# A two-layer trunk with stick-breaking attention: pairs of heads summed at once, gated outputs' low halves on GpSimd, side products dealt by VectorE's work, 72 z products one chunk later

## The chip, the cores and the metric

The kernel runs on one core of one Trainium2 chip. The metric is the time of one execution on the device, in microseconds. An execution has TensorE (PE, with its weight loads PEld), VectorE (DVE), ScalarE (ACT), GpSimd (POOL) and the DMA queue of SyncE (SP). Each engine takes its instructions in order and waits by semaphore.

## What is computed

Two layers on a sequence of 2048 tokens, 1024 channels, all in float32. Layer A is a pooling mixer with a SiLU gate, then an output projection, a residual and a gated embedding add. Layer B is attention with 16 heads of 64 channels. Keys and values come from a projection of the stream after layer A. For layer B, cut to what matters here:

```python
h = rms_norm(x, b_norm[j])
q, z = jnp.split(h @ b_w_in[j], 2, axis=-1)
q = rms_norm(split_heads(q), b_q_norm[j])
# A[t,s] = beta[t,s] * prod_{s<j<t} (1 - beta[t,j]), beta = sigmoid(q.k / sqrt(d)), s < t
o = stick_breaking_attention(q, k_sh, v_sh)
x = x + (o * jax.nn.silu(z)) @ b_w_out[j]
x = x + (p[i] @ ple_w[i]) * jax.nn.sigmoid(x @ ple_gate_w[i])
```

## The kernel before

**Products in two halves.** Every operand of a product with a weight is kept as a pair: a rounded high half and a low half, the rest that the rounding left. A product is three matmuls for each 128 channels of depth: high by high, low by high, high by low (`piecewise`, L990). So each such operand costs a copy on ScalarE (the high half) and a subtraction on VectorE or GpSimd (the low half).

**First part, up to about 1333 us.** Layer A and the projections to q, k and v run for the four chunks of 512 tokens one after the other. Their results go to memory. The change leaves this part as it is: the instructions of every engine keep their order there.

**Second part, the attention.** The four chunks of queries are taken from the last to the first (chunk 3 to chunk 0). In a chunk the heads 0 to 15 follow each other, and for a head the key chunks from its own down to 0. One (query chunk, head, key chunk) is a slot; each slot has four steps, one for each 128 queries. There are 640 steps, numbered n through the loop at L1133: chunk 3 has steps 0 to 255, chunk 2 the steps 256 to 447, chunk 1 the steps 448 to 575, chunk 0 the rest. A head has 16, 12, 8 or 4 steps.

A step does this, in three places of the program:

- `front` (L917): two matmuls give 128x512 logits (L924, L925), ScalarE takes the sigmoid (L928), and VectorE makes the running product along the keys with a scan (L936; for the head's own key chunk L933, where only the keys up to the queries' tile count, so that its four steps are 128, 256, 384 and 512 wide). The scan's two inputs both lie in SBUF.
- six steps later, `turn` (L943): four transposes on TensorE (L949) into one of two PSUM buffers `psa`, a rounded copy by ScalarE (L952) and the low half by VectorE (L953), which reads the PSUM buffer and frees it.
- two steps after that, `gather` (L956): two matmuls (L961, L962) add to the head's output in PSUM (`pso`).

**The end of a head.** A PSUM output holds two 64-row halves that have to be added. One step after the head's last gather, ScalarE copies one half to its place in `os` (L976), and a step later VectorE adds the other half from PSUM (L977). After the odd head of a pair, `gated` adds a vector to the pair with four ScalarE instructions (L972) and GpSimd multiplies by silu(z) (L974). Later `pair_up` (L1000) makes the pair's high half on ScalarE (L1005) and its low half on VectorE (L1006).

**Side products.** Between the steps the loop takes matmuls from a second stream, `filler`, at a fixed number a step (L1152 to L1155). In chunk 3 these are the z products of all four chunks (`gate_z`, L1009: 192 matmuls for a query chunk, 8 groups of 24, and for each group one VectorE multiplication at L1026 and one GpSimd multiplication at L1031). In chunk 2 it is `post(3)` (L1041): chunk 3's output projection (192 matmuls), then its gate and embedding (8 groups of 31). In chunk 1 it is `post(2)`, in chunk 0 `post(1)`, and after the last step `post(0)` runs alone, as the tail. When a chunk's eighth pair is done, 14 steps after its last, what is left of the stream is flushed and the next stream begins (L1166 to L1173). `soon(k, ...)` puts a piece of work k steps later; `stay` holds an instruction at its place in the written order.

Of the kernel before, what the change touches and what calls it, by code (L numbers as in the profile page):

```python
# [15 lines left out]
P = 128  # L16
# [6 lines left out]
W5 = 512  # L23
# [12 lines left out]
def trunk_kernel(ctx, tc, x, xt, pt0, wut, cols, heads, zin, grp, aout, agate, aple,  # L36
# [819 lines left out]
    with ExitStack() as st:  # L856
# [99 lines left out]
        def gather(st, kt):  # L956
# [6 lines left out]
            if st["last"] and kt == 3:  # L963
                half, os, c, h2 = st["h"] % 2, st["os"], st["c"], st["h"] // 2
                mine, other = slice(half * HD, (half + 1) * HD), slice((1 - half) * HD, (2 - half) * HD)

                def gated():
                    zt = t2.tile([P, W5], F32, tag="zt", name="zt", bufs=1)
                    nc.sync.dma_start(out=zt, in_=zd[c][h2])
                    for j in range(4):  # L970
                        js = slice(j * P, (j + 1) * P)
                        stay(A.activation(out=os[:, js], in_=os[:, js], func=AF.Identity,  # L972
                                          bias=ends[c][:, h2, j : j + 1]))
                    G.tensor_tensor(out=os, in0=os, in1=zt, op=ALU.mult)  # L974

                soon(1, lambda: stay(A.copy(out=os[mine], in_=po[other])))  # L976
                soon(2, lambda: V.tensor_tensor(out=os[mine], in0=po[mine], in1=os[mine], op=ALU.add))  # L977
# [22 lines left out]
        def pair_up(c):  # L1000

            if len(ogs[c]) < len(outs[c]):
# [3 lines left out]
                soon(1, lambda: V.tensor_tensor(out=pr[:, 1], in0=os, in1=f(pr[:, 0]), op=ALU.subtract))  # L1006
# [31 lines left out]
        POSTZ = 8 * 24  # L1038
        POST = 8 * 24 + 8 * 31 + 2
# [59 lines left out]

        def beside(c):  # L1100

            if c < NSUB - 1:
                yield from post(c + 1)
                return
            for cz in range(c, -1, -1):
                yield from gate_z(cz)
# [11 lines left out]
        rate = POSTZ / 64.0 - AHEAD * LAG_T / 256.0  # L1118
# [3 lines left out]
        def begin(i):  # L1122
            c, h, kc = slots[i]
            if kc == c:
                if h == 1:
                    early["ends"] = load_ends(c)
                os = head["os"] if h % 2 else t2.tile([P, W5], F32, tag="os", name="os", bufs=9)
                head.clear()
                head.update(q=early.pop("q", None) or load_q(c, h), carry=[None] * 4, o=[], os=os)
# [3 lines left out]
        for n in range(4 * len(slots) + LAG_G):  # L1133
# [18 lines left out]
            owed += rate + (AHEAD if n < LAG_T else 0)  # L1152
# [13 lines left out]
            for c in range(NSUB - 1, 0, -1):  # L1166
                if len(outs[c]) == 8 and c not in done:
# [4 lines left out]
                    rate = POST / (64.0 * c - (LAG_G + 2 if c == 1 else 1))  # L1172
# [57 lines left out]
```

## Time and profile before

| | |
|---|---|
| median of 3 runs | 2716.79 us (2716.16 to 2717.45) |
| the profiled execution, its own time | 2715.51 us |
| its span, first to last instruction | 2713.6 us |
| granted TensorE clock, mean | 0.999 |
| busy over the span | PE 2681.3 us (99%), PEld 2224.8 (82%), DVE 1967.6 (73%), ACT 1365.9 (50%), POOL 874.5 (32%) |
| DMA | 581.55 MB, 214 GB/s |

The profile counts from the span's start. Its stages: the first part 0 to 1333 us, chunk 3 to 1835, chunk 2 to 2183, chunk 1 to 2432, chunk 0 to about 2600, the tail to the end. A row of the windows view gives the busy time of each engine in a stretch. PE's busy time is a union of matmuls whose ends are modelled and which lie over the next one's start, so that a short stop of TensorE does not show in it in full; PEld, the weight loads, is the second witness. A row of a group view ends with the idle time that the engine had just before such instructions, and with what ended it.

### The profile page before, as it was taken

Reading aid. Unit: us, or ns where it says so; the run is one execution under the profiler, and the core shown is the slowest. Engines: PE = TensorE matmul, PEld = TensorE weight load, DVE = VectorE, ACT = ScalarE, POOL = GpSimd, SP = SyncE. Lnnn points to the kernel's source line nnn. Section 1 sums busy time; section 2 is a strip of 40 time slices with the busy share of each in tenths; the row PEclk is TensorE's granted clock in tenths of the full one; section 3 lists DMA queues with packets and bytes.
Section 4 is the critical chain, followed back from the end, with each engine's and each line's share of the span. In section 5 each row is a group of like instructions: output and inputs, shape, how many; then the busy total and the mean of one; then the engine's idle time right before and its main releaser. Section 6 shows DMA issues by size and latency. Waiting matters only on the chain.

```text
span 2713.6 us, 38599 instructions
## 1 busy us (share of the span) xinstructions
PE 2681.3 (99%) x13352; PEld 2224.8 (82%) x13352; DVE 1967.6 (73%) x2565; ACT 1365.9 (50%) x2671; POOL 874.5 (32%) x695
## 2 busy tenths in 40 slices
PE   9999999999999999999999999999999999999999
PEld 8888888888888888888888888887887778888877
DVE  6776626665367643765499999999999998997632
ACT  5445513455135642445365666666666665655430
POOL 3675238642485325753211111110110111112220
PEclk9999999999999999999999999999999999999999
DMA  8657785567846677445679665555555566668865
GB/s 326 225 179 274 249 297 188 208 232 261 295 169 239 222 259 274 136 157 188 201 246 289 187 221 166 169 171 164 178 158 160 164 198 203 197 197 261 268 226 171
DMA packets 276543, 581.55 MB, mean 214 GB/s; under 512 B 33110, under 2 KB 66902, under 8 KB 276348
## 3 DMA queue, kind: packets, MB, share of 16 engines
q1 hardware_dynamic: 270610, 571.41, 63.9%
q10 hardware_dynamic: 5738, 7.68, 1.0%
q8 instruction: 106, 1.74, 0.3%
q14 instruction: 89, 0.73, 0.1%
HBM read 438.40 MB, written 132.19 MB: 210 GB/s over the span
## 4 chain that ended last, share of the span: by engine, by line
PE 85%; DVE 10%; issue 2%; DMA 2%; ACT 1%; POOL 0%; SPq 0%; ACTq 0%; DVEq 0%; POOLq 0%
PE psd L614 19%; PE psd L166 9%; PE psd L167 9%; PE psd L168 9%; PE psa L949 7%; PE psd L993 5%; PE psd L995 5%; PE psd L997 5%; DVE pp L936 5%; PE pso L962 3%; PE psl L925 3%; PE pso L961 3%; PE psl L924 3%; DVE at L953 3%; PE pst L719 1%
## 5 line engine op out<-in xcount | busy, mean ns | idle before, releaser
L952 ACT CAST at<-psa 128x512 fp32r<-128x512 f32 (+3 forms) x640 | 334.8, 523 | 480.4 <-PE psa L949 463.8
L614 PE MATMUL psd<-wpair,x 128*128 128x512 f32 x2304 | 536.8, 391 | 0.0
L936 DVE TENSOR_TENSOR_SCAN pp<-kap,pp,zeros 128x512 f32<-128x512 f32 x384 | 514.2, 1339 | 3.1 <-ACT kap L928 2.4
L614 PEld LDWEIGHTS psd<-wpair,x 128*128 128x128 f32 x2304 | 429.8, 188 | 87.1
L953 DVE TENSOR_TENSOR at<-psa,at 128x512 fp32r<-128x512 f32 (+3 forms) x640 | 380.9, 595 | 83.2 <-ACT at L952 80.3
L949 PE MATMUL psa<-ident,pp 128*128 128x128 f32 x2176 | 346.9, 275 | 21.4 <-DVE at L953 20.2
L928 ACT ACTIVATE kap<-psl 128x512 f32<-128x512 f32 (+3 forms) x640 | 345.2, 539 | 14.2 <-PE psl L925 11.2
L949 PEld LDWEIGHTS psa<-ident,pp 128*128 128x128 f32 x2176 | 262.8, 140 | 98.1 <-DVE at L953 45.8
L924 PE MATMUL psl<-kk,qa 128*128 128x512 f32 (+3 forms) x640 | 281.9, 441 | 0.0
L962 PE MATMUL pso<-at,vv 128*128 128x512 f32 (+3 forms) x640 | 234.7, 367 | 0.8 <-DVE at L953 0.8
L925 PE MATMUL psl<-kk,qb 128*128 128x512 f32 (+3 forms) x640 | 232.7, 364 | 0.0
L961 PE MATMUL pso<-at,vv 128*128 128x512 f32 (+3 forms) x640 | 231.9, 362 | 0.0
L933 DVE TENSOR_TENSOR_SCAN pp<-kap,ahead 128x128 f32<-128x128 f32 (+3 forms) x256 | 223.0, 871 | 5.3 <-ACT kap L928 3.9
L167 PE MATMUL psd<-xp,wpair 128*128 128x512 f32 x512 | 199.4, 390 | 1.5 <-DVE xp L316 1.5
L166 PE MATMUL psd<-xp,wpair 128*128 128x512 f32 x512 | 199.9, 391 | 0.0
L168 PE MATMUL psd<-xp,wpair 128*128 128x512 f32 x512 | 199.2, 389 | 0.0
L149 DVE SCALAR_TENSOR_TENSOR wpair<-wraw,gains,wpair 128x512 fp32r<-128x512 f32 x192 | 161.4, 882 | 45.8 <-ACT wpair L148 45.1
L1031 POOL TENSOR_TENSOR zr<-zr,sgz 128x512 f32<-128x512 f32 x32 | 58.9, 1840 | 370.0 <-ACT sgz L1030 326.9
L143 POOL TENSOR_TENSOR wpair<-wraw,wpair 128x512 fp32r<-128x512 f32 x99 | 144.4, 1468 | 81.2 <-ACT wpair L141 76.6
L148 ACT ACTIVATE wpair<-wraw,gains 128x512 fp32r<-128x512 f32 x192 | 132.9, 718 | 69.3 <-DMA wraw<-in_bq_dram 29.6
L141 ACT CAST wpair<-wraw 128x512 fp32r<-128x512 f32 x148 | 89.7, 618 | 119.5 <-PE psd L168 91.4
L962 PEld LDWEIGHTS pso<-at,vv 128*128 128x128 f32 x640 | 120.2, 188 | 27.9 <-DVE at L953 1.5
(194 smaller groups left out, 5318.8 us busy)
## 6 DMA issues: line engine op xcount, KB each, us to landing
kk<-kd SPq DMA_DIRECT2D x320, 128.0 KB
vv<-vd SPq DMA_DIRECT2D x160, 256.0 KB
wraw<-in_kv_dram SPq DMA_DIRECT2D x128, 256.0 KB
wpair<-wzd SPq DMA_DIRECT2D x64, 512.0 KB
wpair<-wod SPq DMA_DIRECT2D x64, 512.0 KB
wpair<-wgd SPq DMA_DIRECT2D x64, 512.0 KB
wpair<-wu SPq DMA_DIRECT2D x48, 512.0 KB
wpair<-wi SPq DMA_DIRECT2D x36, 512.0 KB
```

What stands on the lines that cost most here:

```text
L166: T.matmul(ps, wst(units, kt, 0, c0), acts[kt][:, 0], start=(begin and kt == order[0]), stop=False)
L167: T.matmul(ps, wst(units, kt, 0, c0), acts[kt][:, 1], start=False, stop=False)
L168: T.matmul(ps, wst(units, kt, 1, c0), acts[kt][:, 0], start=False, stop=(end and kt == order[-1]))
L614: T.matmul(pss2[i], ck["x2"][kt][:, xh, tk], wst(ws, kt, wh, 0, W5), start=(kt == 0 and xh == 0 and wh == 0), stop=(kt == KT - 1 and wh == 1))
L924: T.matmul(ps[:, :w], qa[:, qs], kk[:, :w], start=True, stop=False)
L925: T.matmul(ps[:, :w], qb[:, qs], kk[:, :w], start=False, stop=True)
L928: A.activation(out=kp[:, r0:], in_=ps[:, :w], func=AF.Sigmoid, scale=-1.0)
L936: V.tensor_tensor_scan(out=pp[:, ::-1], data0=kp[:, ::-1], data1=zeros.to_broadcast([P, W5]), initial=st["carry"][j], op0=ALU.mult, op1=AL ...
L949: T.transpose(pt[:, j * P : (j + 1) * P], pp[:, r0 + kt * P : r0 + (kt + 1) * P], ident)
L952: A.copy(out=at[:, 0, cs], in_=pt[:, cs])
L953: V.tensor_tensor(out=at[:, 1, cs], in0=pt[:, cs], in1=f(at[:, 0, cs]), op=ALU.subtract)
L962: T.matmul(po[:, cs], vv[:, kt, :], at[:, 1, cs], start=False, stop=(st["last"] and kt == 3))
```

## The change

Four edits, all in the attention part.

**Heads.** At the end of a head both halves are now copied from PSUM by ScalarE: the half in the wrong rows to a second buffer `ob` (L976), the other to `os` (L977). VectorE adds only once for a pair of heads, 128x512 from SBUF and SBUF (L979), in place of two additions of 64x512 from PSUM and SBUF. `gated` comes one step later than before.

**Low halves.** `pair_up`'s subtraction is on GpSimd (L1007), but for the two that fall in the tail, which stay on VectorE.

**Side products dealt.** In chunks 3 and 2 the number of side products of a step is no longer fixed. `shares` works out from the widths of a step's scan and low half a time for VectorE, and from its matmuls one for TensorE, and gives each step as many side products as bring TensorE's time to k times VectorE's, at least 0.5; k is found so that the sum is right. The dealing goes on to 14 steps past the chunk's last (step 269, then 461). Chunks 1 and 0 keep a fixed number.

**72 products later.** The z products of chunk 0 are begun in chunk 3 as before, but 72 of their 192 matmuls (3 of 8 groups) are left over and come first in chunk 2. Chunk 3 then has 696 side products in place of 768, chunk 2 has 514 in place of 442.

```diff
             if st["last"] and kt == 3:
-                half, os, c, h2 = st["h"] % 2, st["os"], st["c"], st["h"] // 2
+                half, os, ob, c, h2 = st["h"] % 2, st["os"], st["ob"], st["c"], st["h"] // 2
...
-                soon(2, lambda: V.tensor_tensor(out=os[mine], in0=po[mine], in1=os[mine], op=ALU.add))
+                soon(1, lambda: stay(A.copy(out=ob[mine], in_=po[other])))
+                soon(2, lambda: stay(A.copy(out=os[mine], in_=po[mine])))
                 if half:
-                    soon(3, gated)
+                    soon(3, lambda: V.tensor_tensor(out=os, in0=os, in1=ob, op=ALU.add))
+                    soon(4, gated)
                     soon(6, lambda: outs[c].append(os))
...
-                soon(1, lambda: V.tensor_tensor(out=pr[:, 1], in0=os, in1=f(pr[:, 0]), op=ALU.subtract))
+                soon(1, lambda: (V if tail[0] else G).tensor_tensor(
+                    out=pr[:, 1], in0=os, in1=f(pr[:, 0]), op=ALU.subtract))
...
+        HELD = 3 * 24
...
+        last_z = gate_z(0)
...
         def beside(c):
...
+            if c == NSUB - 1:
+                for cz in range(c, 0, -1):
+                    yield from gate_z(cz)
+                for _ in range(POSTZ - HELD):
+                    next(last_z)
+                    yield
                 return
...
+            if c == NSUB - 2:
+                yield from last_z
+            yield from post(c + 1)
...
+        def widths(n, lag):
+            i, j = divmod(n - lag, 4)
+            if not 0 <= i < len(slots):
+                return 0
+            c, _, kc = slots[i]
+            return (4 if kc < c else (j + 1 if not lag else 4 - j)) * P
...
+        def shares(n0, n1, total):
+            scan, turned_, gathered = ([widths(n, lag) for n in range(n0, n1)] for lag in (0, LAG_T, LAG_G))
+            vector = [(0.15 + 0.0022 * a if a else 0.0) + (0.14 + 0.00105 * t if t else 0.0) for a, t in zip(scan, turned_)]
+            tensor = [2 * max(0.109, 0.2265 * a / W5) * (a > 0) + 0.109 * t / P + 2 * max(0.109, 0.2265 * g / W5) * (g > 0)
+                      for a, t, g in zip(scan, turned_, gathered)]
+            part = lambda k: [max(0.5, (k * v - t) / 0.2265) + (AHEAD if n0 + i < LAG_T else 0)
+                              for i, (v, t) in enumerate(zip(vector, tensor))]
...
-        rate = POSTZ / 64.0 - AHEAD * LAG_T / 256.0
+        share, even = shares(0, stops[NSUB - 1], NSUB * POSTZ - HELD), 0.0
...
-            owed += rate + (AHEAD if n < LAG_T else 0)
+            owed += even or share.get(n, 0.0)
...
-                    rate = POST / (64.0 * c - (LAG_G + 2 if c == 1 else 1))
+                    if c == NSUB - 1:
+                        share = shares(n + 1, stops[c - 1], POST + HELD)
+                    else:
+                        even = POST / (64.0 * c - (LAG_G + 2 if c == 1 else 1))
```

Two places where the order of instructions moves. The first is TensorE at the passage from chunk 3 to chunk 2. `xz` is the z products' input, so a row with `xz` is a side product; L924 with 128x128 is the first step of chunk 2. Before, TensorE has there:

```order
L993 MATMUL psd<-xz,wpair 128x512
L995 MATMUL psd<-xz,wpair 128x512
L997 MATMUL psd<-xz,wpair 128x512
L961 MATMUL pso<-at,vv 128x512
L962 MATMUL pso<-at,vv 128x512
L949 MATMUL psa<-ident,pp 128x128 x4
L924 MATMUL psl<-kk,qa 128x128
L925 MATMUL psl<-kk,qb 128x128
L961 MATMUL pso<-at,vv 128x512
L962 MATMUL pso<-at,vv 128x512
L949 MATMUL psa<-ident,pp 128x128 x4
L924 MATMUL psl<-kk,qa 128x256
```

Now it has, a little further on in the same head, from its second step:

```order
L924 MATMUL psl<-kk,qa 128x256
L925 MATMUL psl<-kk,qb 128x256
L998 MATMUL psd<-xz,wpair 128x512
L961 MATMUL pso<-at,vv 128x512
L962 MATMUL pso<-at,vv 128x512
L949 MATMUL psa<-ident,pp 128x128 x4
L924 MATMUL psl<-kk,qa 128x384
L925 MATMUL psl<-kk,qb 128x384
L994 MATMUL psd<-xz,wpair 128x512
L996 MATMUL psd<-xz,wpair 128x512
```

Before, the side products end with the last step of chunk 3, and the first ones of the next stream come 14 steps later; now nearly every step from there on has one to four.

The second place is ScalarE at the end of an odd head of chunk 2. `kap` is the sigmoid's output, L952 the rounded copy that VectorE's L953 needs. Before:

```order
L976 COPY os<-pso 64x512
L952 CAST at<-psa 128x128
L928 ACTIVATE kap_12443<-psl 128x512
L952 CAST at<-psa 128x512
L928 ACTIVATE kap_12444<-psl 128x512
L972 ACTIVATE os<-os,en 128x128 x4
```

Now, at the end of such a head:

```order
L976 COPY ob<-pso 64x512
L952 CAST at<-psa 128x128
L928 ACTIVATE kap_12443<-psl 128x512
L977 COPY os<-pso 64x512
L952 CAST at<-psa 128x512
L928 ACTIVATE kap_12444<-psl 128x512
L952 CAST at<-psa 128x512
L928 ACTIVATE kap_12445<-psl 128x512
L972 ACTIVATE os<-os,en 128x128 x4
```

One more copy stands ahead of a step's L952, and the four instructions of `gated` come one step later.

More of the change, by code (lines that the diff above doesn't have):

```diff
@@ L1117, in trunk_kernel @@
         AHEAD = 4
-        rate = POSTZ / 64.0 - AHEAD * LAG_T / 256.0
+        stops = {}
+        for n, (c, _, _) in enumerate(slots):
+            stops[c] = 4 * (n + 1) + LAG_G + 6
+        share, even = shares(0, stops[NSUB - 1], NSUB * POSTZ - HELD), 0.0
         done = set()
@@ L1127, in begin @@
                 os = head["os"] if h % 2 else t2.tile([P, W5], F32, tag="os", name="os", bufs=9)
+                ob = head["ob"] if h % 2 else t2.tile([P, W5], F32, tag="ob", name="ob", bufs=1)
                 head.clear()
[L1129 removed]
+                head.update(q=early.pop("q", None) or load_q(c, h), carry=[None] * 4, o=[], os=os, ob=ob)
             kk = early["k"].pop(0) if early["k"] else load_k(kc, h)
```

10 lines of the change are left out of this document (5 added, 5 removed).

## The prediction

> **What bounds the kernel now.** I read the page's busy times first, then the windows view, cut at the chunks of the attention, with chunk 2 (1835 to 2183) cut in three. Each of its rows gives, after a stretch's length, the busy time and count of PE, PEld, DVE, ACT and POOL.
>
> ```profile
> PE 2681.3 (99%) x13352; PEld 2224.8 (82%) x13352; DVE 1967.6 (73%) x2565; ACT 1365.9 (50%) x2671; POOL 874.5 (32%) x695
> ```
>
> ```profile
> 1333.00:1835.00 502.00, 496.77 (x2701) 412.98 (x2700) 473.36 (x565) 300.90 (x599) 76.55 (x44) 1.00 0.66 205
> 1835.00:1860.00 25.00, 21.14 (x121) 15.46 (x120) 24.91 (x32) 17.80 (x38) 2.56 (x2) 1.00 0.65 198
> 1860.00:2032.00 172.00, 171.52 (x957) 143.11 (x956) 169.96 (x213) 111.58 (x229) 24.14 (x13) 1.00 0.53 163
> 2032.00:2183.00 151.00, 142.64 (x779) 115.67 (x778) 148.58 (x185) 93.19 (x191) 11.52 (x8) 1.00 0.53 163
> 2183.00:2432.00 249.00, 245.27 (x1350) 205.02 (x1349) 230.93 (x305) 150.40 (x329) 37.17 (x24) 1.00 0.66 202
> 2432.00:2600.00 168.00, 167.68 (x892) 141.42 (x891) 118.90 (x184) 82.70 (x202) 35.41 (x24) 1.00 0.83 253
> ```
>
> TensorE is the bound nearly everywhere: it is idle for 5.2, 3.9, 0.5, 8.4, 3.7 and 0.3 us, 22.0 in all. VectorE is nearly full in chunk 2 (24.91 of 25, 148.58 of 151). Next the waits view of the attention, TensorE's two rows: what waited, for what, us, times, longest.
>
> ```profile
> PEld psa L949 <- DVE at L953: 45.8, 72, 2.6
> PE psa L949 <- DVE at L953: 20.2, 35, 2.2
> ```
>
> So one thing stops TensorE: a transpose finds no free PSUM buffer because VectorE has not yet taken the low half out of it. The matmul view understates these stops, since a row's end lies over the next start. Three stretches without a stop show it by the weight loads:
>
> ```profile
> 1500.00:1725.00 225.00, 225.00 (x1233) 188.22 (x1232) 211.91 (x254) 135.83 (x269) 32.27 (x18) 1.00 0.58 185
> 1862.00:1955.00 93.00, 92.92 (x517) 77.80 (x518) 91.69 (x116) 59.97 (x123) 12.30 (x7) 1.00 0.56 174
> 2220.00:2350.00 130.00, 130.00 (x720) 110.15 (x719) 118.90 (x155) 77.80 (x170) 21.50 (x13) 1.00 0.66 198
> ```
>
> Where TensorE never stops, PEld is busy 188.22/225 = 0.8365 of the time, 0.847 in chunk 1. A stretch's PEld over that share is its full work: 493.7 of 502, 18.5 of 25, 171.1 of 172, 138.3 of 151, 242.0 of 249. By this the idle time is 8.3, 6.5, 0.9, 12.7 and 7.0, with chunk 0's 0.3 together 35.7 us. The Trainium skill, "Perfetto Trace Analysis", section "Identifying the Most-Contended Engine", says the same of the witness: judge TensorE's headroom by weight-load time, not by matmul busy time. By that page alone PEld's 82 to 84% would promise a sixth of the span; the trace disagrees, since 0.8365 is what a stretch without any stop has.
>
> The change keeps every one of the 13352 matmuls. What it can win is therefore these 22 to 36 us, no more.
>
> **z products, 72 of them, and the dealing.** A side product's price, from a stretch of ten back to back in the tail, first and last:
>
> ```profile
> 2610.77 0.40 PE L993 MATMUL psdt<-og,wpair 128*128 128x512 f32 x1
> ...
> 2612.82 0.39 PE L993 MATMUL psdt<-og,wpair 128*128 128x512 f32 x1
> ```
>
> Nine intervals take 2.05 us, 0.228 each. So 72 x 0.228 = 16.4 us of TensorE's work leave chunk 3 and enter chunk 2: on the sum nothing, unless they land where TensorE stood idle. They do: in 1835 to 1860, 14 steps, TensorE had no side products at all, and is given some 37 (8.4 us) against 3.9 to 6.5 us idle. I count that idle as gone but for 0.5 to 1. Chunk 1's first 14 steps likewise get some 37 of chunk 2's.
>
> The rest depends on VectorE's demand beside TensorE's. These are VectorE's rows of chunk 2, by form, and the last the scan of chunk 3:
>
> ```profile
> L936 DVE TENSOR_TENSOR_SCAN pp<-kap,pp,zeros 128x512 f32<-128x512 f32 x128 | 171.9, 1343 | 0.3 <-ACT kap L928 0.2
> L977 DVE TENSOR_TENSOR os<-pso,os 64x512 f32<-64x512 f32 x16 | 10.8, 678 | 0.2
> L1006 DVE TENSOR_TENSOR og<-os,og 128x512 fp32r<-128x512 f32 x7 | 5.6, 806 | 0.0
> L1085 DVE TENSOR_TENSOR sg<-sg,x 128x512 f32<-128x512 f32 x6 | 4.0, 660 | 0.0
> L1026 DVE TENSOR_TENSOR zr<-psd,rb 128x512 f32<-128x512 f32 x1 | 0.7, 657 | 0.0
> ...
> L936 DVE TENSOR_TENSOR_SCAN pp<-kap,pp,zeros 128x512 f32<-128x512 f32 x192 | 257.8, 1343 | 2.6 <-ACT kap L928 2.3
> ```
>
> **Heads.** Sixteen additions (10.8 us) become eight. Before has no such addition; the nearest rows with two SBUF inputs and this shape are L1085 (0.660) and, stretched at times, L1006 (0.806). I take 0.70: 5.6 us, so 5.2 saved a chunk (bounds 4.4 and 5.5).
>
> **Low halves on GpSimd.** Eight a chunk leave VectorE, 8 x 0.806 = 6.4 us. They don't leave it wholly. One place, with what GpSimd does beside:
>
> ```profile
> 2157.82 1.29 POOL L1084 TENSOR_TENSOR sg<-sg,x 128x512 f32<-128x512 f32 x1 [25.22 <-DVE sg L1083]
> 2158.26 1.93 DVE L936 TENSOR_TENSOR_SCAN pp<-kap,pp,zeros 128x512 f32<-128x512 f32 x1
> 2159.06 2.19 POOL L974 TENSOR_TENSOR os<-os,zt 128x512 f32<-128x512 f32 x1
> 2160.11 1.68 DVE L1006 TENSOR_TENSOR og<-os,og 128x512 fp32r<-128x512 f32 x1
> 2162.45 0.66 PE L949 MATMUL psa<-ident,pp 128*128 128x128 f32 x4 [2.19 <-DVE at L953]
> ```
>
> And the durations of scan and low half over all steps, minimum, median and maximum in ns:
>
> ```profile
> L936 DVE TENSOR_TENSOR_SCAN pp<-kap,pp,zeros x384: 1262/1275/2330, 1341.7 to 2432.6; 128x512 f32<-128x512 f32 x192
> L953 DVE TENSOR_TENSOR at<-psa,at x640: 257/659/694, 1345.8 to 2609.3; 128x512 fp32r<-128x512 f32 x160
> ```
>
> Beside GpSimd the scan takes 1.93 in place of its median 1.275, L1006 1.68, and TensorE stops for 2.19 us. The two rows above show who is hit: the scan, both inputs in SBUF, goes up to 2.33; L953, one input in PSUM, never past 0.69. The Trainium skill, "GPSIMD Engine Reference", section "Key points", has this as a rule: GpSimd shares its SBUF interfaces with VectorE and contends with instructions of two SBUF inputs. The trace agrees by 2.33 against 0.69. It speaks against this change twice: more GpSimd work beside the scans, and L977, with a PSUM input, gives way to an addition that can be hit.
>
> The mean price: scans exceed their median by 1.343 - 1.275 = 0.068; times 128 that is 8.7 us in chunk 2, over GpSimd's 23 instructions 0.38 each; chunk 3's scans have the same mean, 192 x 0.068 = 13.1 over 44, 0.30. I take 0.33. Eight low halves give back 2.6 of the 6.4 us (worst, all at 2.33 - 1.275 = 1.06: 8.5, a loss of 2.1).
>
> **VectorE after.** Chunk 3 with the 14 steps behind it (1333 to 1860): 473.4 + 24.9 - 5.2 - 3.8 (low halves, net), and three groups of z fewer at 0.66 + 0.33 each, -3.0: 486 us. TensorE: 512 to 518 - 16.4 = 496 to 501. Ratio 0.97 to 0.98. The rest of chunk 2 (1860 to 2183): 318.5 less some 8 of the 9, and 3.0 more: 313; TensorE 309 to 314, with 72 - 37 side products 8 more, 317 to 322: 0.97 to 0.99, where it was 1.01 to 1.03. What such ratios leave idle, the rows of before tell: chunk 3 with 0.953 to 0.959 had 5.2 to 8.3 us in 502 (1.0 to 1.7%), 1860 to 2032 with 0.99 had 0.3 to 0.5%, 2032 to 2183 with 1.04 to 1.07 had 5.5 to 8.4%. The limit is near 1, and both stretches come to lie under it. So chunk 3 keeps 5 to 7, the rest of chunk 2 falls to 3.5 to 5, chunk 1 (VectorE 9 us less) from 3.7 or 7.0 to 2.3 or 4, chunk 0 keeps 0.3.
>
> **ScalarE's copies.** One more of 0.581 a head, 37 us on its queue. What covers it:
>
> ```profile
> L976 ACT COPY os<-pso 64x512 f32<-64x512 f32 x62 | 36.0, 581 | 1.5
> ```
>
> ScalarE's longest wait in chunk 3 and in chunk 2, by the waits view:
>
> ```profile
> ACT at L952 <- PE psa L949: 175.8, 213, 1.6
> ACT at L952 <- PE psa L949: 116.3, 148, 3.2
> ```
>
> Ahead of L952 ScalarE itself waits for TensorE, 175.8/213 = 0.83 us on average in chunk 3 and 0.79 in chunk 2, longer than a copy. Hidden there, I count nothing. In the tail it isn't: the last pair's chain runs bare.
>
> ```profile
> 2609.99 0.58 ACT L976 COPY os<-pso 64x512 f32<-64x512 f32 x1 [2.20 <-PE pso L962]
> 2610.79 0.69 DVE L977 TENSOR_TENSOR os<-pso,os 64x512 f32<-64x512 f32 x1
> 2614.87 0.73 PE L993 MATMUL psdt<-og,wpair 128*128 128x512 f32 x2 [0.53 <-ACT og L1005]
> ```
>
> TensorE already waits 0.53 there. A second copy ends at 2611.15 in place of the 2610.79 at which the addition began: +0.4.
>
> **Sum.** By the matmul view 22.0 becomes 5 + 0.5 + 3.5 + 2.3 + 0.3 = 11.6, by the weight loads 35.7 becomes 7 + 1 + 5 + 4 + 0.3 = 17.3: -10.4 and -18.4, middle -14.4, tail +0.4: -14.0. The profiled execution took 2715.5; its span is 2713.6 and 1.9 lie around it. 2715.5 - 14.0 = 2701.5; the median of the runs is 1.3 above that execution: **2702.8**. A difference under 0.2% (5.4 us) is about what a measurement here cannot tell from none.
>
> **Rivals.** *Nearly all idle goes* (0.20): with dealing that follows VectorE's load, both chunks run like 1860 to 2032, 0.5%, and keep 4 of 18.0 to 28.4; chunk 1 keeps 2: 6 of 22 or 36 left, -16 to -30, about 2694. For it: that stretch did so at 0.99.
>
> *GpSimd's contention eats the gain* (0.14): each low half stretches a scan by the full 1.06. VectorE then has 319 in the rest of chunk 2, 0.99 to 1.0, and 490 in chunk 3, 0.98 to 0.99; idle as midway between the 0.99 and the 1.04 stretch in chunk 2, 3% (10), and as in chunk 3 before in chunk 3, 1.7% (8): with 3.2 and 0.3 elsewhere 21.5 in place of 28.9, the middle of 22.0 and 35.7. Some 7 are won: 2710. Against it: the mean price is 0.33.
>
> *The gate moves* (0.08): chunk 3 at its higher ratio takes the idle share that chunk 2 had as a whole, 12.7 of 348 or 3.6%, on 500 us 18 in place of 7, while chunk 2 wins 12 and chunk 1 two: 2714, within 0.2%.
>
> *ScalarE in the way, slower* (0.06): the extra copies put L952 back, so L953, so the next transposes. In chunks 3, 2 and 1 that is 48 x 0.581 = 27.9 us against the 14 won: 2731. It decides once ScalarE's wait before L952 is shorter than 0.58 at the heads' ends.
>
> The forecast has 0.52. The range takes it, most of the first two rivals and their bounds: 2692 to 2712. Faster by over 0.2% (below 2711.4): 0.52 + 0.20 + 0.10 of the second = 0.82; the rest of it and the third 0.12; slower 0.06.
>
> **What would show it.** Right: in the new profile 14 steps after chunk 3's end PE is full; chunk 3 is 20 to 27 us shorter, chunk 2 up to 9 and chunk 1 up to 7 longer, with waits of L949 on L953 about halved in times; L977's 0.68 gone, L936's mean at 1.34 to 1.37. Wrong: waits of L953 for L952 in chunks 3 and 2 beyond some 30 us (the copies), a scan mean past 1.40 (contention), or L949's waits as many as before.

## The result and the profile after

The kernel after takes 2702.36 us (median of six runs), the kernel before beside it 2717.12: a ratio of 0.9945 [0.9932, 0.9957], 14.8 us less. One of the six runs took 9225.38 us at a granted clock of 0.279; the ratio leaves it out, and the median of the other five is 2702.04. The profiled execution took 2702.7 us, its span is 2700.8 (before 2713.6), with 1.9 around it as before. Its granted clock is 1.000 (before 0.999).

The page's busy times first, then the windows view of after, cut where after reaches the steps 256, 270, 448, 462 and 576: chunk 3, the 14 steps behind it, the rest of chunk 2, the 14 steps behind that, the rest of chunk 1, chunk 0, the tail. After a stretch's length come PE, PEld, DVE, ACT and POOL.

```profile
PE 2675.5 (99%) x13352; PEld 2226.3 (82%) x13352; DVE 1938.8 (72%) x2503; ACT 1399.2 (52%) x2735; POOL 923.9 (34%) x725
```

```profile
1333.00:1812.00 479.00, 473.66 (x2600) 393.22 (x2599) 459.63 (x547) 304.49 (x607) 76.70 (x43) 1.00 0.66 204
1812.00:1837.00 25.00, 25.00 (x147) 21.03 (x145) 23.83 (x31) 17.02 (x37) 5.35 (x3) 1.00 0.52 167
1837.00:2167.00 330.00, 326.15 (x1803) 272.99 (x1802) 320.48 (x388) 216.86 (x443) 63.22 (x35) 1.00 0.57 176
2167.00:2192.00 25.00, 24.98 (x149) 21.05 (x147) 24.21 (x33) 17.60 (x40) 4.23 (x3) 1.00 0.67 197
2192.00:2418.00 226.00, 221.08 (x1215) 185.69 (x1214) 201.08 (x258) 141.66 (x306) 44.24 (x29) 1.00 0.67 202
2418.00:2580.00 162.00, 161.73 (x862) 136.42 (x861) 106.08 (x162) 87.54 (x210) 40.58 (x30) 1.00 0.86 257
2580.00:2701.00 121.00, 113.26 (x505) 91.94 (x503) 33.74 (x50) 22.58 (x45) 17.09 (x13) 1.00 0.60 194
```

Length less PE gives TensorE's idle time by the matmul view; length less PEld over 0.8365 (0.847 in chunks 1 and 0) gives it by the weight loads, as in the prediction. The column of before keeps the prediction's cuts:

| idle, us (matmul view / weight loads) | before | forecast | after |
|---|---|---|---|
| chunk 3 | 5.2 / 8.3 | 5 / 7 | 5.3 / 8.9 |
| the 14 steps behind it | 3.9 / 6.5 | 0.5 / 1 | 0.0 / 0.0 |
| rest of chunk 2 | 8.9 / 13.6 | 3.5 / 5 | 3.9 / 3.7 |
| chunk 1, its first 14 steps too | 3.7 / 7.0 | 2.3 / 4 | 4.9 / 6.9 |
| chunk 0 | 0.3 | 0.3 | 0.3 |
| sum | 22.0 / 35.7 | 11.6 / 17.3 | 14.4 / 19.8 |

The time came from the passage from chunk 3 to chunk 2 (its 14 steps) and from the rest of chunk 2. Chunk 1 is the place that did not follow: its idle time rose where it was to fall. Before, cut at step 270 (1858 us) and step 462 (2208 us) too, shows it:

```profile
1835.00:1858.00 23.00, 19.45 (x112) 14.21 (x110) 22.91 (x28) 16.21 (x35) 2.56 (x2) 1.00 0.63 187
1858.00:2183.00 325.00, 315.85 (x1744) 260.03 (x1743) 320.54 (x401) 206.36 (x423) 35.66 (x21) 1.00 0.53 164
2183.00:2208.00 25.00, 24.30 (x139) 19.59 (x138) 23.02 (x32) 15.99 (x38) 2.59 (x2) 1.00 0.67 195
2208.00:2432.00 224.00, 220.96 (x1214) 185.43 (x1213) 207.92 (x274) 134.41 (x292) 34.58 (x22) 1.00 0.66 203
```

In the rest of chunk 2 VectorE's work stayed the same (320.54, then 320.48), while the matmuls went from 1744 to 1803. TensorE was brought up to VectorE there, not VectorE down to TensorE. The windows view of the side products alone (tile `wpair`; PE's busy time and count) says how far, before and after:

```profile
1858.00:2183.00 325.00, 123.31 (x404) 1.00 0.53 164
1837.00:2167.00 330.00, 137.15 (x473) 1.00 0.57 176
```

That is 69 more, at the prediction's 0.228 us each 15.7 us of TensorE's work. In the 14 steps behind chunk 2 there were 29 side products already before, and there are 32 after. In the rest of chunk 1 VectorE lost 6.8 us of work (207.92, then 201.08) and TensorE stopped longer (3.0, then 4.9).

The waits view of after's attention, TensorE's two rows (what waited, for what, us, times, longest):

```profile
PEld psa L949 <- DVE at L953: 26.1, 40, 1.9
PE psa L949 <- DVE at L953: 12.6, 21, 1.5
```

Times fell from 72 to 40 and from 35 to 21, a little less than halved; the waits that are left still have the same cause. VectorE's scans, the new addition of the heads and the new low halves on GpSimd, in two group views and the view of a line (minimum, median, maximum in ns):

```profile
L936 DVE TENSOR_TENSOR_SCAN pp<-kap,pp,zeros 128x512 f32<-128x512 f32 x384 | 513.4, 1337 | 6.3 <-ACT kap L928 5.4
L979 DVE TENSOR_TENSOR os<-os,ob 128x512 f32<-128x512 f32 x31 | 22.5, 727 | 0.3 <-ACT os L977 0.3
```

```profile
L1007 POOL TENSOR_TENSOR og<-os,og x30: 1288/1678/2231, 1766.4 to 2584.4; 128x512 fp32r<-128x512 f32 x30
```

The mean of these 384 scans did not rise: 1337 ns, before 1339. The 64 narrow scans (L933, 128x128) did, from 476 to 558 ns, 5.2 us in all. In the experiments below they take 480 without relief and 544 with the heads in pairs alone, so most of it comes with the heads. The heads' addition takes 0.727 (0.70 was taken). What rose most is another of VectorE's instructions, the embedding addition at L1085, now L1088, in chunks 2 and 1. First before, then after:

```profile
L1085 DVE TENSOR_TENSOR sg<-sg,x 128x512 f32<-128x512 f32 x13 | 8.7, 668 | 1.8 <-POOL sg L1084 1.8
```

```profile
L1088 DVE TENSOR_TENSOR sg<-sg,x 128x512 f32<-128x512 f32 x14 | 17.9, 1275 | 6.4 <-POOL sg L1087 6.4
```

It takes twice as long, and VectorE stands 6.4 us waiting for the GpSimd addition in front of it (L1087), 1.8 before. One such place in chunk 1, in the timeline of after (start, duration, engine; in brackets the idle time just before):

```profile
2388.94 0.66 DVE L1086 TENSOR_TENSOR sg<-psd,sg 128x512 f32<-128x512 f32 x1
2389.37 1.29 POOL L1007 TENSOR_TENSOR og<-os,og 128x512 fp32r<-128x512 f32 x1 [10.21 <-ACT og L1006]
2390.63 1.28 POOL L1087 TENSOR_TENSOR sg<-sg,x 128x512 f32<-128x512 f32 x1
2391.94 0.69 DVE L1088 TENSOR_TENSOR sg<-sg,x 128x512 f32<-128x512 f32 x1 [2.33 <-POOL sg L1087]
2392.55 0.68 DVE L953 TENSOR_TENSOR at<-psa,at 128x512 fp32r<-128x512 f32 x1
2393.29 0.66 PE L949 MATMUL psa<-ident,pp 128*128 128x128 f32 x4 [0.88 <-DVE at L953]
```

GpSimd had been idle for 10.21 us and got the low half (L1007) just ahead of the addition that VectorE needs (L1087). VectorE, in order, stood 2.33 us before L1088, behind it L953, behind that TensorE's transpose. At other places the low half runs beside L1088 itself, which then takes 1.71 to 1.76 us. The Trainium skill, "GPSIMD Engine Reference", section "Key points", says that GpSimd contends with VectorE's instructions of two SBUF inputs; L1088 has two, and its 1.76 us there against 0.658 at best agree with that.

In the tail, the end of the last pair of heads in the timeline of after:

```profile
2596.81 0.58 ACT L976 COPY ob<-pso 64x512 f32<-64x512 f32 x1 [1.19 <-PE pso L962]
2597.40 0.58 ACT L977 COPY os<-pso 64x512 f32<-64x512 f32 x1
2598.01 0.69 DVE L979 TENSOR_TENSOR os<-os,ob 128x512 f32<-128x512 f32 x1 [0.43 <-ACT os L977]
...
2602.09 0.73 PE L994 MATMUL psdt<-og,wpair 128*128 128x512 f32 x2 [0.94 <-ACT og L1006]
```

From the first copy to the first product 5.28 us; before it was 2614.87 - 2609.99 = 4.88. TensorE waits 0.94 in place of 0.53.

### The profile page after: what moved, and what is told of

Read it like the earlier page. It is cut to its first block, busy times and chain, and to the rows that moved or that the text cites. A ratio compares the mean times of both kernels' runs of the same rounds, so it can differ in the third digit from the quotient of the medians.

```text
span 2700.8 us, 38620 instructions
## 1 busy us (share of the span) xinstructions
PE 2675.5 (99%) x13352; PEld 2226.3 (82%) x13352; DVE 1938.8 (72%) x2503; ACT 1399.2 (52%) x2735; POOL 923.9 (34%) x725
## 5 line engine op out<-in xcount | busy, mean ns | idle before, releaser
L952 ACT CAST at<-psa 128x512 fp32r<-128x512 f32 (+3 forms) x640 | 334.7, 523 | 436.5 <-PE psa L949 427.1
L936 DVE TENSOR_TENSOR_SCAN pp<-kap,pp,zeros 128x512 f32<-128x512 f32 x384 | 513.4, 1337 | 6.3 <-ACT kap L928 5.4
L953 DVE TENSOR_TENSOR at<-psa,at 128x512 fp32r<-128x512 f32 (+3 forms) x640 | 381.4, 596 | 83.7 <-ACT at L952 78.7
L924 PE MATMUL psl<-kk,qa 128*128 128x512 f32 (+3 forms) x640 | 282.3, 441 | 0.3 <-DMA kk<-kd 0.3
L933 DVE TENSOR_TENSOR_SCAN pp<-kap,ahead 128x128 f32<-128x128 f32 (+3 forms) x256 | 227.1, 887 | 5.2 <-ACT kap L928 3.2
```

Of the source, the lines that this page charges most:

```text
L924: T.matmul(ps[:, :w], qa[:, qs], kk[:, :w], start=True, stop=False)
L933: V.tensor_tensor_scan(out=pp[:, r0:][:, ::-1], data0=kp[:, r0:][:, ::-1], data1=ahead[:, r0:][:, ::-1], initial=1.0, op0=ALU.mult, op1=AL ...
L936: V.tensor_tensor_scan(out=pp[:, ::-1], data0=kp[:, ::-1], data1=zeros.to_broadcast([P, W5]), initial=st["carry"][j], op0=ALU.mult, op1=AL ...
L952: A.copy(out=at[:, 0, cs], in_=pt[:, cs])
L953: V.tensor_tensor(out=at[:, 1, cs], in0=pt[:, cs], in1=f(at[:, 0, cs]), op=ALU.subtract)
```

## The experiments

**The theories.** The prediction's: the idle time goes because three things work together, the dealing, the 72 products held over, and VectorE's relief (heads and low halves), without which the two stretches would not come under the ratio 1 (VectorE's busy time over TensorE's). A first rival: the order of the side products does it all, and the relief adds nothing. A second: the relief is worth something, and the low halves on GpSimd cost it again. A third: the gain comes from one of the two changes of order alone. Medians are given with the lowest and the highest run; the kernels ran in three sittings of four, each beside before, whose medians there were 2716.65, 2716.71 and 2718.68 us. Kernels of different sittings, after among them, are compared by their ratios to before or by their spans; each span is that of one profiled execution. Lengths of a few us are those of the profiled spans.

**The order of the side products without relief.** After, with heads and low halves as before:

```diff
-                soon(1, lambda: stay(A.copy(out=ob[mine], in_=po[other])))
-                soon(2, lambda: stay(A.copy(out=os[mine], in_=po[mine])))
+                soon(1, lambda: stay(A.copy(out=os[mine], in_=po[other])))
+                soon(2, lambda: V.tensor_tensor(out=os[mine], in0=po[mine], in1=os[mine], op=ALU.add))
...
-                    soon(3, lambda: V.tensor_tensor(out=os, in0=os, in1=ob, op=ALU.add))
-                    soon(4, gated)
+                    soon(3, gated)
...
-                soon(1, lambda: (V if tail[0] else G).tensor_tensor(
-                    out=pr[:, 1], in0=os, in1=f(pr[:, 0]), op=ALU.subtract))
+                soon(1, lambda: V.tensor_tensor(out=pr[:, 1], in0=os, in1=f(pr[:, 0]), op=ALU.subtract))
```

> The side products are dealt as in the changed kernel and 72 of them held over; the end of a head and the low halves are as before (VectorE adds twice a pair from PSUM, and subtracts). Idle theory (TensorE's stops are what was won; both parts are needed to bring VectorE's demand under TensorE's): the 14 steps behind chunks 3 and 2 are filled, worth 4 to 6 us, but VectorE has 9 us more in each chunk, 0.99 to 1.01 of TensorE's work, so idle stays at 2 to 4% in the rest of chunk 2: 2707 to 2711. Rival, the dealing alone is the gain: 2701 to 2704. Rival, VectorE's relief alone is the gain: 2715 to 2718.

Measured: 2702.58 us (2702.48 to 2704.76), 0.9949 [0.9936, 0.9961]: all of the change's gain. Its windows view, chunk 3, the 14 steps behind, the rest of chunk 2:

```profile
1333.00:1813.00 480.00, 474.80 (x2597) 392.74 (x2597) 465.21 (x556) 296.38 (x592) 69.14 (x40) 1.00 0.66 204
1813.00:1839.00 26.00, 25.14 (x144) 20.60 (x143) 25.59 (x33) 16.67 (x36) 3.41 (x2) 1.00 0.50 158
1839.00:2171.00 332.00, 328.55 (x1813) 273.55 (x1811) 325.64 (x406) 209.57 (x428) 39.99 (x25) 1.00 0.56 176
```

VectorE has 325.64 us to do in the rest of chunk 2, 5.2 more than in after, and TensorE stops there for about as long: 3.5 us by the matmuls (after 3.9), 5.0 by the weight loads (after 3.7), where before had 8.9 and 13.6. So the prediction's theory falls in this point: the relief was not needed for it.

**The relief alone.** Before, with the heads and the low halves of after (the same lines the other way round, put on the kernel before):

```diff
-                soon(1, lambda: stay(A.copy(out=os[mine], in_=po[other])))
-                soon(2, lambda: V.tensor_tensor(out=os[mine], in0=po[mine], in1=os[mine], op=ALU.add))
+                soon(1, lambda: stay(A.copy(out=ob[mine], in_=po[other])))
+                soon(2, lambda: stay(A.copy(out=os[mine], in_=po[mine])))
...
-                soon(1, lambda: V.tensor_tensor(out=pr[:, 1], in0=os, in1=f(pr[:, 0]), op=ALU.subtract))
+                soon(1, lambda: (V if tail[0] else G).tensor_tensor(
+                    out=pr[:, 1], in0=os, in1=f(pr[:, 0]), op=ALU.subtract))
```

> Heads summed in pairs and low halves on GpSimd as in the changed kernel; side products at a fixed number a step and none held over, as before. Idle theory: the 14 steps behind chunk 3 stay without side products and idle 3.5 to 6 us; VectorE's 9 us less bring chunk 2 from 1.02-1.05 of TensorE's work to 1.00-1.02, so its later part idles some 4 us less: 2711 to 2714. Rival, relief alone is the gain: 2701 to 2704. Rival, dealing alone is the gain: 2715 to 2718.

Measured: 2710.81 (2709.91 to 2712.24), 0.9978 [0.9969, 0.9987], just under the first theory's range. Alone the relief is worth some 6 us; on top of the order of the side products it is worth nothing (0.9945 with it, 0.9949 without). The rest of chunk 1 in its windows view:

```profile
2200.00:2426.00 226.00, 221.38 (x1216) 185.62 (x1215) 201.89 (x259) 142.27 (x308) 44.65 (x30) 1.00 0.66 201
```

Idle 4.6 in place of before's 3.0: the loss in chunk 1 comes with the relief, in this order of the side products as in after's.

**72 products held over, nothing else.** Before, with fixed rates:

```diff
+        HELD = 3 * 24
+        last_z = gate_z(0)
...
+            if c == NSUB - 1:
+                for cz in range(c, 0, -1):
+                    yield from gate_z(cz)
+                for _ in range(POSTZ - HELD):
+                    next(last_z)
+                    yield
...
+            if c == NSUB - 2:
+                yield from last_z
+            yield from post(c + 1)
...
-        rate = POSTZ / 64.0 - AHEAD * LAG_T / 256.0
+        rate = (4 * POSTZ - HELD) / 256.0 - AHEAD * LAG_T / 256.0
...
-                    rate = POST / (64.0 * c - (LAG_G + 2 if c == 1 else 1))
+                    rate = (POST + (HELD if c == NSUB - 1 else 0)) / (64.0 * c - (LAG_G + 2 if c == 1 else 1))
```

> The kernel before with one edit: 72 of chunk 0's z products come first in chunk 2 in place of last in chunk 3, at a fixed number a step in both chunks (2.72 and 2.69). No dealing past a chunk's end, heads and low halves as before. Idle theory: the 14 steps behind chunk 3 stay empty (3.5 to 6 us idle stay), but in the rest of chunk 2 TensorE's work rises to 326 to 331 against VectorE's 323, a ratio of 0.98 to 0.99 in place of 1.01 to 1.03, so that its 9 to 14 us of idle fall to 2 to 5: 2707 to 2711. Rival, holding them over is all of the gain: 2701 to 2704. Rival, it is worth nothing without dealing by work: 2715 to 2718.

Measured: 2710.98 (2708.91 to 2713.72), 0.9979 [0.997, 0.9988]. Its windows:

```profile
1333.00:1824.00 491.00, 482.45 (x2631) 400.92 (x2630) 464.79 (x558) 298.07 (x594) 68.78 (x41) 1.00 0.65 202
1824.00:1846.00 22.00, 18.40 (x110) 14.08 (x108) 21.91 (x29) 15.15 (x33) 1.27 (x1) 1.00 0.50 151
1846.00:2178.00 332.00, 329.49 (x1813) 273.75 (x1812) 325.17 (x407) 210.08 (x429) 42.95 (x25) 1.00 0.56 174
```

The rest of chunk 2 is cured (9.2 us idle, now 2.5), the passage is not (3.6), and chunk 3 has lost 3.3 (5.2, now 8.5), with fewer side products there at a fixed rate. With the dealing (first experiment) chunk 3 has the 5.2 again; what in the fixed rate loses them was not shown. VectorE has 325.17 us in the rest of chunk 2, before 320.54: the products held over bring work for VectorE too, which the relief takes off again in after (320.48).

**The dealing, nothing else.** The first experiment's kernel with none held over:

```diff
-        HELD = 3 * 24
+        HELD = 0
```

> The kernel before with the dealing alone: by VectorE's work and over the 14 steps behind a chunk, none held over, heads and low halves as before. Idle theory: the filled steps win 4 to 6, but the rest of chunk 2 is left with VectorE's 318 against TensorE's 301 to 306, a ratio of 1.04 to 1.06, which idles 17 to 22 us in place of 9 to 14: 2714 to 2718. Rival, dealing by itself is worth a part, whatever is held: 2707 to 2711.

Measured: 2706.84 (2705.48 to 2707.68), 0.9955 [0.9943, 0.9968]. The idle theory's range was wrong by 7 us or more, the rival's by 0.2. The windows say why:

```profile
1333.00:1823.00 490.00, 486.86 (x2663) 406.50 (x2662) 468.74 (x561) 300.33 (x597) 73.75 (x43) 1.00 0.66 206
1823.00:1850.00 27.00, 26.35 (x151) 21.73 (x150) 26.37 (x34) 16.79 (x37) 3.39 (x2) 1.00 0.58 176
1850.00:2175.00 325.00, 315.68 (x1737) 260.62 (x1736) 319.25 (x399) 206.54 (x423) 39.02 (x22) 0.99 0.55 167
```

The passage is filled (0.7 us idle), chunk 3 stops for 3.1, and the rest of chunk 2 stays at 9.3, as in before (9.2): nearly the same matmuls (1737 and 1744) beside the same 319 to 321 us of VectorE's work. So the two changes of order cure different places, and the spans add up: dealing -7.7, held over -4.4, both -12.3 (2701.3 against 2713.6). The ratios alone would not carry that sum, since each is uncertain by about 3 us.

**After with none held over**, the same edit on after:

```diff
-        HELD = 3 * 24
+        HELD = 0
```

> The changed kernel with all 192 z products of chunk 0 in chunk 3, still dealt by VectorE's work and over the 14 steps behind it. Idle theory: 16.4 us of TensorE's work go back from chunk 2 to chunk 3; in chunk 2 VectorE has 310 us against TensorE's 301 to 306, a ratio of 1.01 to 1.03, which idles 2 to 4%, 5 to 10 us more than the changed kernel: 2707 to 2712. Rival, where the 72 stand is of no matter as long as the edges are filled: 2701 to 2704.

Measured: 2711.19 (2709.74 to 2715.02), 0.998 [0.9971, 0.9989]. The rest of chunk 2 in its windows:

```profile
1847.00:2171.00 324.00, 313.61 (x1741) 260.39 (x1740) 317.09 (x385) 214.19 (x439) 50.86 (x29) 1.00 0.54 168
```

10.4 us idle, although VectorE is relieved: with 317.09 us it still has more to do than TensorE's 313.61. Held-over products are what this stretch needs.

**Low halves back on VectorE.** After, with the heads in pairs kept:

```diff
-                soon(1, lambda: (V if tail[0] else G).tensor_tensor(
-                    out=pr[:, 1], in0=os, in1=f(pr[:, 0]), op=ALU.subtract))
+                soon(1, lambda: V.tensor_tensor(out=pr[:, 1], in0=os, in1=f(pr[:, 0]), op=ALU.subtract))
```

> The changed kernel with the gated outputs' low halves back on VectorE. By the mean price (a low half on GpSimd gives VectorE 0.81 us and takes 0.33 by stretched scans): VectorE has some 4 us more in each chunk, idle grows by 1 to 3: 2703 to 2706. Rival, contention costs as much as it saves (in the changed kernel's chunk 2 the addition of the embedding takes 1184 ns in place of 660 and waits for GpSimd): 2699 to 2702.

Measured: 2698.14 (2697.93 to 2699.04), 0.9931 [0.9919, 0.9944]. This is below both ranges. Its span is 5.1 under that of the kernel without relief and 4.6 under that of after. The intervals of the ratios overlap, but no run of the kernel without relief, in the same sitting, came below 2702.48. The rest of chunk 2, that of chunk 1, and the embedding addition:

```profile
1837.00:2167.00 330.00, 327.28 (x1808) 273.09 (x1807) 321.89 (x399) 217.09 (x443) 41.21 (x25) 1.00 0.57 177
2191.00:2414.00 223.00, 221.16 (x1221) 186.34 (x1219) 203.11 (x266) 142.00 (x307) 34.43 (x22) 1.00 0.69 206
```

```profile
L1087 DVE TENSOR_TENSOR sg<-sg,x 128x512 f32<-128x512 f32 x14 | 10.4, 744 | 3.0 <-POOL sg L1086 3.0
```

Idle in chunk 1 1.8 in place of 4.9, with 2 us more of work on VectorE; the addition at 744 in place of 1275. The theories' second rival is right by this: the heads' pairing is worth about 5 us, the low halves on GpSimd give it back.

**Low halves three steps later**, to take them out of the way on GpSimd:

```diff
-                soon(1, lambda: (V if tail[0] else G).tensor_tensor(
+                soon(4, lambda: (V if tail[0] else G).tensor_tensor(
```

> The changed kernel with GpSimd's low halves put four steps after the high half in place of one. The low halves on GpSimd cost 4.2 us (the changed kernel against the one with them on VectorE). If the cost is that they stand beside GpSimd's embedding addition and VectorE's one behind it (L1087, L1088: 1.71 us in place of 0.66, or a wait of 0.8 to 2.3): most of it comes back, 2698 to 2700. Rival, the cost is that of any GpSimd work beside the scans: no change, 2702 to 2704.

Measured: 2701.57 (2699.79 to 2702.75), 0.9942 [0.993, 0.9955]. The instructions of every engine came out in the same order as in after, so it tests nothing of the order; it is another measurement of after (0.9945). The addition's row is after's too: 1277 ns, 6.4 us of waiting.

**Low halves apart from the embedding.** The pair's two halves are made nine side products into the next group of the gate's products, no longer at a group's end, where the embedding addition stands:

```diff
-                yield from piecewise(ps, wg, x3, 0)
+                for item, _ in enumerate(piecewise(ps, wg, x3, 0)):
+                    if c and o and item == 8:
+                        pair_up(c - 1)
+                    yield
...
-                if c:
+                if c and o == KT - 1:
                     pair_up(c - 1)
```

> The changed kernel, low halves on GpSimd, but in the gate part of a chunk a pair's high half is made nine side products into the next group in place of at the group's end, so that GpSimd's low half runs well apart from its embedding addition (L1090) and VectorE's addition behind it (L1091). If the 4.2 us that GpSimd's low halves cost come from standing ahead of that addition in GpSimd's queue or beside VectorE's: waits of VectorE's addition fall from 6.4 to some 3 us and its mean from 1275 to about 750 ns in chunks 2 and 1, and the time to 2697 to 2700. Rival, the cost is spread over the scans: 2701 to 2704.

Measured: 2695.66 (2695.00 to 2698.39), 0.9917 [0.9904, 0.9931]: the best of all kernels run, its interval just clear of after's [0.9932, 0.9957], and below the range expected. The addition's wait fell further than expected and its mean (892) less. Its addition, the rests of chunks 2 and 1, and one place in the timeline:

```profile
L1091 DVE TENSOR_TENSOR sg<-sg,x 128x512 f32<-128x512 f32 x14 | 12.5, 892 | 1.8 <-POOL sg L1090 1.8
```

```profile
1835.00:2163.00 328.00, 326.26 (x1808) 273.75 (x1806) 318.77 (x388) 216.98 (x443) 60.34 (x35) 1.00 0.57 178
2188.00:2411.00 223.00, 220.14 (x1212) 185.30 (x1211) 203.00 (x258) 141.56 (x306) 45.78 (x29) 1.00 0.68 204
```

```profile
2372.18 1.29 POOL L1007 TENSOR_TENSOR og<-os,og 128x512 fp32r<-128x512 f32 x1 [3.43 <-ACT og L1006]
...
2384.40 1.29 POOL L1090 TENSOR_TENSOR sg<-sg,x 128x512 f32<-128x512 f32 x1 [8.76 <-DVE sg L1089]
2386.42 0.66 DVE L1091 TENSOR_TENSOR sg<-sg,x 128x512 f32<-128x512 f32 x1
```

Here the low half lies 12 us ahead of the next embedding addition. In chunks 2 and 1 GpSimd's low half now starts 1 to 8 us behind its embedding addition and 11 or more ahead of the next; in after, 6 of these 16 low halves stood directly ahead of that addition and most of the others directly behind it, many of them beside L1088. VectorE's wait for GpSimd is back at 1.8 and the idle times are 1.7 and 2.9 (after 3.9 and 4.9). The work on GpSimd is the same as in after. So it was the place, not the amount. The pair's high half, a copy on ScalarE, moved along with the low half, and no run moves the low half alone. Whether this is also better than the low halves on VectorE stays open: the spans say 2.6 us, the intervals overlap.

**The same sums dealt evenly.** After, with each chunk's side products spread over the same steps in equal numbers:

```diff
-            return dict(zip(range(n0, n1), part(hi)))
+            early_ = sum(AHEAD for n in range(n0, n1) if n < LAG_T)
+            return {n: (total - early_) / (n1 - n0) + (AHEAD if n < LAG_T else 0) for n in range(n0, n1)}
```

> The changed kernel with the same sums dealt over the same steps, but the same number in each step (2.49 in chunk 3, 2.68 in chunk 2) in place of numbers that follow VectorE's work. Idle theory with elastic buffers (a scan may lag some steps behind): VectorE falls behind in a head's full steps and catches up in its four narrow ones, little is lost: 2702 to 2706. Rival, dealing by work is what made it: 2708 to 2713.

Measured: 2705.82 (2703.79 to 2706.02), 0.9956 [0.9944, 0.9969]; beside it on the same chip the kernel with after's order took 2701.57 (2699.79 to 2702.75). So of the 14.8 us won some 3 to 4 hang on dealing by VectorE's work (3.2 by the spans, 4.2 by the medians; the intervals overlap), and 2702 to 2706, the first theory's range, fits. The rest of the dealing's worth is that it reaches past chunk 3's end: the 14 empty steps are filled here too, with no idle time.

**A copy more on ScalarE.** After, with the first copy of each head's end done twice (64 x 0.58 = 37 us more on ScalarE):

```diff
                 soon(1, lambda: stay(A.copy(out=ob[mine], in_=po[other])))
+                soon(1, lambda: stay(A.copy(out=ob[mine], in_=po[other])))
```

> The changed kernel with a third ScalarE copy at each head's end: the copy to ob is made twice, which adds 64 copies of 0.58 us, 37 us on ScalarE's queue. If ScalarE's own wait for TensorE covers a copy: 2702 to 2704. Rival, each copy puts the low half and the next transposes back: up to 28 us, 2710 to 2730.

Measured: 2703.87 (2702.55 to 2704.88), 0.9952 [0.9938, 0.9965], 2.3 more than the kernel beside it, in spans nothing (2700.8, as after). ScalarE's wait for the transposes takes it up, first in after, then here:

```profile
ACT at L952 <- PE psa L949: 427.1, 519, 2.3
```

```profile
ACT at L952 <- PE psa L949: 397.9, 472, 2.2
```

29 us less waiting for 37 us more work. The rival with ScalarE in the way, at up to 28 us for such a copy, is ruled out.

**96 held over in place of 72**, on the kernel with the low halves on VectorE:

```diff
-        HELD = 3 * 24
+        HELD = 4 * 24
```

> The changed kernel with low halves on VectorE (2698.1) and 96 products held over in place of 72. Idle theory: 5.5 us more of TensorE's work in chunk 2, both chunks near a ratio of 0.98 already, so nothing or little is left to win: 2696 to 2700. Rival, chunk 3's remaining 5 us of idle are VectorE's and go with it: 2693 to 2695. Rival, chunk 2's flow breaks: over 2701.

Measured: 2700.22 (2698.85 to 2700.37), 0.9931 [0.9917, 0.9944], the ratio that 72 had. Chunk 3 and the rest of chunk 2:

```profile
1333.00:1808.00 475.00, 469.66 (x2582) 389.02 (x2581) 459.46 (x548) 303.24 (x606) 68.74 (x39) 1.00 0.65 203
1832.00:2168.00 336.00, 332.80 (x1828) 276.91 (x1827) 324.21 (x400) 217.93 (x444) 40.98 (x26) 1.00 0.57 176
```

The rest of chunk 2 has 332.80 of 336 busy, 3.2 idle (327.28 of 330, 2.7, with 72). With 24 more matmuls held over, 5.5 us, this stretch is 6 us longer and chunk 3 only 4 shorter (475 us; with 72 held over 479). TensorE was over VectorE in this stretch already (327.28 to 321.89 with 72), so more matmuls only make it longer.

**Chunk 1 dealt by VectorE's work too**, on the same kernel:

```diff
-                    if c == NSUB - 1:
-                        share = shares(n + 1, stops[c - 1], POST + HELD)
+                    if c > 1:
+                        share = shares(n + 1, stops[c - 1], POST + (HELD if c == NSUB - 1 else 0))
```

> The changed kernel with low halves on VectorE (2698.1), and chunk 1's side products too dealt by VectorE's work and over the 14 steps behind it. Chunk 1 has 1.8 to 3 us of idle left in that kernel: 2696 to 2698. Rival, the 14 steps of chunk 0 are no better a place, as TensorE is full there, and the next stream begins later: 2698 to 2700.

Measured: 2702.88 (2702.62 to 2705.38), 0.9944 [0.9931, 0.9956]. The rest of chunk 1:

```profile
2193.00:2420.00 227.00, 223.22 (x1224) 187.07 (x1223) 202.48 (x266) 141.27 (x306) 33.43 (x22) 1.00 0.66 202
```

This is outside both ranges. The stretch takes 227 us in place of 223, idle 3.8 in place of 1.8: worse. Its span is 5.4 us longer than without this dealing, but 2.0 of these lie in the first part, where the order is the same, and the intervals overlap. VectorE has 202 us there beside TensorE's 223, so it is not the limit of the stretch; why dealing by its work does harm was not settled.

## Why the prediction was right, and where its steps were not

**Bound and size.** The forecast was 2702.8 us, measured were 2702.36. TensorE's idle time as the whole of what can be won held: its matmuls are still 13352, and idle time fell by 7.6 us in the matmul view and 15.9 by the weight loads, against 10.4 and 18.4. The profiled execution came down by 12.8 us, forecast 14.0. The truth lies nearer to the weight loads here: less 1.0 for the tail they give 14.9, the matmul view 6.6. The forecast took the middle of the two views, and by the idle times measured that middle gives only 10.8. So two errors met: the idle time that stays was forecast too low, and the middle counts too little of what was won. That 14.0 came out beside 12.8 is in part luck.

**The passage.** Right: 3.9 to 6.5 us idle, now none. It got 31 side products (some 37 were forecast). The dealing does it, as the kernel with only the dealing shows.

**Chunk 3 and the rest of chunk 2.** Right in size (5.3 and 3.9 us of idle time, forecast 5 and 3.5), wrong in cause. The step that failed is "VectorE after", with "the limit is near 1, and both stretches come to lie under it" by way of some 9 us taken off VectorE. Two of its terms were off and made up for each other in the ratio. VectorE was to fall from 318.5 to 313 in the rest of chunk 2 and stayed at 320.5. TensorE was to get "72 - 37" products, 8 us, and got 69, 15.7 us: the 37 of "Chunk 1's first 14 steps likewise get some 37" are hardly new, since 29 stood there before and 32 do after. So the ratio of 0.97 to 0.99 came out (320.48 to 326.15 is 0.98), but by TensorE's work. The kernel without any relief has VectorE at 325.64 beside TensorE's 328.55 and the same 3.5 idle. The products held over raise TensorE's work to VectorE's; that alone cures this stretch. That the ratio decides was right for it, and the kernels with none held over show it: with 319 to 316 (or 317 to 314) the stretch keeps 9 to 10 us. In the rest of chunk 1 it does not decide: at 201 to 221 after idles longer than before at 208 to 221.

**The low halves.** The mean price of 0.33 us on the scans was the wrong price at the wrong place. Against the kernel with the low halves on VectorE all scans together take 2.5 us more in after, 0.08 for each of the 30 low halves. The cost lies at the places, eight a chunk, where the low half stands ahead of, or beside, the embedding's step: over the attention L1088 takes 24.7 us in place of 17.3 and waits 17.1 in place of 9.3. TensorE feels it in chunk 1 above all: idle time 4.9 where 2.3 was forecast, which with 2.6 is nearly all that the idle sum was off (14.4 against 11.6). In spans the low halves cost 4.6 us; moved apart, their high halves with them, they cost nothing. The rival of GpSimd's contention was nearer in size (it has 7 us lost), but by another way than stretched scans.

**The heads.** Priced as relief, 5.2 us a chunk off VectorE. They are worth about 5 us in all, spread by about 1 us over the stretches (the kernel without relief against the one with the low halves on VectorE). The forecast counted heads and low halves together as relief; measured, 5 us won by the one and 4.6 lost by the other cancel, and all of the gain is left to the order of the side products.

**ScalarE's copies.** Right: hidden, even with a third one. In the tail the chain grew by 0.40, as forecast; the tail's stretch grew from 120.0 to 121.0 by the windows, and the rest of that, some 0.6 us, was not traced.

**Rivals.** "Nearly all idle goes" would need chunk 3 and the rest of chunk 2 to keep 4 us by the middle of the views; they keep 9 to 13. "The gate moves" did not happen in the change; a part of it shows in the kernel with only the products held over, where chunk 3 idles 8.5 us (the rival has 18).

## What to carry to other kernels

When two engines are both near full in a stretch, compare their work stretch by stretch, and first move work that the waiting engine can do into the stretch, from one where it is the limit: here that won 12 us, with as many matmuls as before. Work that goes to an engine with idle time goes into that engine's queue: look at what stands right behind it there, and who waits for that, before taking a mean price. When a forecast of several edits fits, run each edit alone: two terms that cancel look like two that are right.

## What the runs showed of the hardware

A VectorE addition of two 128x512 SBUF inputs (L1088) took 0.658 us at best and up to 1.76 beside a GpSimd instruction of the same shape; VectorE's L953, with one input in PSUM, never took more than 0.694 over 640 instructions. GpSimd's low half took 1.29 us at its shortest and 2.23 at its longest. That the 384 long scans took no harm from 30 more GpSimd instructions (mean 1337 ns, before 1339) was not expected.
